# PSUM instead of SBUF for the gathered tokens' rows and sums and for the dense activations; three shared two-bank tiles for the sums over U and V

## The chip, the cores and the metric

One core of one Trainium2 chip runs the whole kernel. The metric is the device time of one execution in microseconds (us). Five engines work side by side, each with its own queue that it executes in order: TensorE (PE; its weight loads are listed as PEld), VectorE (DVE), ScalarE (ACT), GpSimd (POOL) and SyncE (SP), which only issues transfers. Sixteen DMA engines move data between HBM and SBUF. Matrix products are written to PSUM, which has eight banks of 128 partitions x 512 float32; DVE and ACT also read and write PSUM.

## What is computed

The reference is one decoder block over 1024 tokens of 1024 features: RWKV-7 time mixing and sparse attention side by side, merged through gates, a first LayerNorm, then a channel mixer (PEER) and a second LayerNorm. The change lies in PEER, which picks 128 of 16384 single-neuron experts for each token (8 heads x 16) and adds them up:

```
def chunk(args):                       # h2 rows, chosen experts, gates
    hc, ec, gc = args
    act = gelu(einsum('cd,chkd->chk', hc, u_tab[ec])) * gc
    return einsum('chk,chkd->cd', act, v_tab[ec])
x = layer_norm(ALPHA * x + gt2 * y2, ln2_g, ln2_b)
```

## The kernel before, in words

Instructions are written as Python generators over tiles; a planner then lays out the order of each engine's queue when the kernel is built, by its own costs of the instructions, and puts in the waits. A tile pool gives each name a fixed number of slots; an instruction that needs a slot waits until the last user of the slot's former tile is done.

Up to about 1650 us run the projections, RWKV, the attention and the first LayerNorm (twice, for 512 tokens each). Then come two stages in which PEER is computed in two ways at once:

- The 384 first tokens (NG = 3 tiles of 128) are **gathered** (`peer_gather`). For each of a token's 128 experts an indirect transfer, issued by POOL (L1366), brings one row of U per partition, 128 x 1024 float32, into a tile `g`, and DVE multiplies it with the tokens' rows `gh2` and sums (L1370) into one column of `dots`. After 128 such rows GELU and gates are applied, and 128 rows of V follow, which DVE adds up, each times its column of `dots`, into `gacc` (L1372 for the first, L1374 for the others). `g` has three slots, and one more (`g2`) in the last stage. `finish` multiplies `gacc` by gt2 (L1412), adds the residual (L1423), and normalizes. The U rows of tile 0 are taken before 1650 us, spread between RWKV's steps.
- The other 640 tokens (DN) are **dense**: they go through all 16384 experts, 128 at a time. `dots_u` multiplies a block of U with `h2T`; `dense_u` takes GELU (L1305, L1308), multiplies by the gates' table `gt` (L1309), and splits the result into a rounded part and the rest (a copy at L229, then L1312), `A`; `dense_v` multiplies eight of those by a block of V and adds to `yacc` (L1323). Each block of weights is loaded as `raw`, rounded by ACT (`whi`, L229), and POOL takes the rest (`wlo`, L1272). Products are made of three float32r matmuls per slice (`mm6`), for two halves of 320 tokens: 48 matmuls for each block.

The first of the two stages (about 1650 to 2395 us) is the retrieval of the tiles left and the tables of gates (`gate_table`, L1247, L1252), with V rows of the gathered tile 0, and with the products of 69 of the 128 blocks of U ("ahead"), which are stored in HBM (`dotD`). The second (about 2395 to 4007 us) is the dense part proper: groups of eight blocks of U, where the ahead ones come back from HBM into `al`, and the eight V products of the group before are emitted after the first four of a group. The gathered tiles 1 and 2 run beside it. After the last group `fin1` normalizes the dense tokens.

PSUM before is one pool for the whole kernel: `acc` two banks, `rw` four, `tp` two. A dense U block takes two `rw` banks until GELU has read them into `al` (SBUF); a V block takes one `acc` and one `tp` until L1323 has read them. So two U blocks and two V blocks have room at a time.

Of the kernel before, what the change touches and what calls it, by code (L numbers as in the profile page):

```python
# [8 lines left out]
F32 = mybir.dt.float32  # L9
F32R = mybir.dt.float32r  # L10
# [27 lines left out]
ONV = (2, 7)        # tiles whose scores are counted on VectorE  # L38
# [23 lines left out]
# candidate pairs (a, b) of ranks that can be among the 16 largest sums: (a+1)(b+1) <= 16  # L62
# [3 lines left out]
# ---------------------------------------------------------------- constants of the shapes alone  # L66
# [10 lines left out]
def _consts():  # L77
# [43 lines left out]
    # places where the ranks of the first key begin among the candidates, their differences, the ranks  # L121
# [26 lines left out]
def layout(i):  # L148
    """Data layout only: transposes, splits and joins of the inputs."""
# [55 lines left out]
def body(tc, a, out, dbg=None, ntiles=8, mark=lambda s: None):  # L205
# [25 lines left out]
    # ------------------------------------------------------------ modulation: first its part for h  # L231
# [10 lines left out]
    modc = base.tile([128, 48], F32, name="modc")     # sh1, 1 + sc1, gt1 / 2, shift and scale of h2, gt2  # L242
# [32 lines left out]
    def mod_rest(mp):  # L275
        """gt1 as columns; h2 = xn * scale + shift, as columns and as rows; gt2 as both."""
# [46 lines left out]
    def mod_row(dst, n):  # L323
        """The n-th row of shift and scale of h2, gt2, ALPHA times those of the first LayerNorm."""
# [3 lines left out]
    # ------------------------------------------------------------ constants, small parameters  # L328
# [40 lines left out]
        # rows of heads spread over their features, times the weights of the group norm  # L369
# [9 lines left out]
    # relative bias, negated and relative to the last bucket, as tiles over (query, key) of the last 256 keys  # L379
# [26 lines left out]
    def split_w(src, n):  # L406
        """A weight tile as the sums of pairs of float32r tiles, 512 columns each."""
# [11 lines left out]
    def proj(pt, w, act, nk):  # L419
        """pt[128 cols, n] = sum over k tiles, with weights and activations split in two."""  # L420
# [24 lines left out]
    xaD = [tc.dram_tile([128, 1024], F32, name=f"xaD{i}") for i in range(NGT)]  # L445
    h2D = [tc.dram_tile([128, 1024], F32, name=f"h2D{i}") for i in range(NGT)]
# [18 lines left out]
    def kv_index(H, act_of, zp, after=lambda: None):  # L465
        """c_kv, k_idx and w_idx (tokens on partitions) and q_idx; act_of(k) gives slice k of h, split in two."""
# [52 lines left out]
    def zphase1(H, hh, zp, side, pace):  # L519
        """Decay, gates and the rows of RWKV; pace steps of side are emitted after each column tile."""  # L520
# [5 lines left out]
        def shifted(j, dst):  # L526
            """Column tile j, mixed with the token before."""
# [10 lines left out]
        # decay (tokens on partitions), a, and what the output's gate is made of  # L538
# [13 lines left out]
        # k, r and v  # L552
# [35 lines left out]
        def norm():  # L588
            """kk over its norm, and what follows from it."""
# [14 lines left out]
    def spread():  # L604
        """What spreads rows of heads over their features."""
# [4 lines left out]
    def zphase2(H, act, js, side=iter(())):  # L610
        for j in js:
# [7 lines left out]
            else:  # L619
                # twice the sigmoid, less one  # L620
# [4 lines left out]
    anchors = [[], [], []]      # of RWKV for each half of the tokens and of the second merge: instructions of VectorE, in turn, that other work is queued behind  # L625
# [1067 lines left out]
```

## Time and profile before

| | |
|---|---|
| median of 3 runs | 4005.12 us (3998.66 to 4007.22) |
| span of the profiled execution | 4007.3 us |
| PE busy | 3605.5 us (90%), 24045 matmuls |
| DVE busy | 3036.1 us (76%) |
| POOL busy | 2236.6 us (56%) |
| ACT busy | 1618.8 us (40%) |
| moved by DMA | 924.65 MB, mean 231 GB/s |
| mean granted TensorE clock | 0.939 |

The span is that of one execution, from the first to the last instruction; no time of that execution besides its span was recorded. Busy time is the union of the engine's instructions; matmuls are pipelined, so a record of 310 ns can follow the one before after 147 ns. [...]

### The profile page before, as it was taken

Reading aid. Unit: us, or ns where it says so; the run is one execution under the profiler, and the core shown is the slowest. Engines: PE = TensorE matmul, PEld = TensorE weight load, DVE = VectorE, ACT = ScalarE, POOL = GpSimd, SP = SyncE. Lnnn points to the kernel's source line nnn. Section 1 sums busy time; section 2 is a strip of 40 time slices with the busy share of each in tenths; the row PEclk is TensorE's granted clock in tenths of the full one; section 3 lists DMA queues with packets and bytes.
Section 4 is the critical chain, followed back from the end, with each engine's and each line's share of the span. In section 5 each row is a group of like instructions: output and inputs, shape, how many; then the busy total and the mean of one; then the engine's idle time right before and its main releaser. Section 6 shows DMA issues by size and latency. Waiting matters only on the chain.

```text
span 4007.3 us, 65204 instructions
## 1 busy us (share of the span) xinstructions
PE 3605.5 (90%) x24045; PEld 3208.2 (80%) x24045; DVE 3036.1 (76%) x6103; ACT 1618.8 (40%) x3034; POOL 2236.6 (56%) x1566
## 2 busy tenths in 40 slices
PE   8698999888999998888988999999899999898997
PEld 6477776665777776678988889998899989898997
DVE  7556654857367758899999995887788877877874
ACT  3448942343444443564554654222222222222223
POOL 5342222345455543235455455777877777787775
PEclk9898998988999999889999999999999999999998
DMA  6463324855666665477777688888888888888873
GB/s 227 122 192 96 102 91 138 279 185 185 196 216 214 216 217 154 141 270 263 248 252 255 239 266 311 296 283 286 296 304 290 302 283 281 291 289 287 289 261 116
DMA packets 438172, 924.65 MB, mean 231 GB/s; under 512 B 36596, under 2 KB 198588, under 8 KB 434908
## 3 DMA queue, kind: packets, MB, share of 16 engines
q1 hardware_dynamic: 315132, 502.04, 38.1%
q0 software_dynamic: 122720, 418.43, 31.2%
q8 instruction: 190, 3.11, 0.3%
q14 instruction: 130, 1.06, 0.1%
HBM read 792.64 MB, written 127.68 MB: 230 GB/s over the span
## 4 chain that ended last, share of the span: by engine, by line
PE 39%; DVE 25%; DMA 14%; issue 10%; POOL 7%; ACT 3%; SPq 1%; POOLq 0%; DVEq 0%; ACTq 0%
DMA g<-in_u_dram,gidx 5%; PE acc L425 4%; PE acc L426 4%; PE acc L427 4%; DVE gacc L1374 4%; DVE g L1370 3%; POOL g L1366 3%; POOL wlo L1272 3%; DVE gt L1252 3%; DMA g<-in_v_dram,gidx 2%; DMA al<-dotD 2%; PE rw L1289 2%; PE rw L1287 2%; PE rw L1285 2%; PE acc L1287 2%
## 5 line engine op out<-in xcount | busy, mean ns | idle before, releaser
L1272 POOL TENSOR_TENSOR wlo<-raw,whi 128x1024 fp32r<-128x1024 f32 x264 | 662.2, 2509 | 162.2 <-ACT whi L229 156.0
L1366 POOL DMA_INDIRECT g<-in_v_dram,gidx x384 | 504.5, 1314 | 381.7 <-DVE gacc L1374 179.2
L415 POOL TENSOR_TENSOR wlo<-wraw,whi 128x512 fp32r<-128x512 f32 x280 | 374.3, 1340 | 606.2 <-ACT whi L229 537.2
L1370 DVE SCALAR_TENSOR_TENSOR g<-g,gh 128x1024 f32<-128x1024 f32 x384 | 570.5, 1505 | 173.6 <-DMA g<-in_u_dram,gidx 172.8
L1366 POOL DMA_INDIRECT g<-in_u_dram,gidx x384 | 509.4, 1326 | 343.6 <-DVE g L1370 210.0
L1374 DVE SCALAR_TENSOR_TENSOR gacc<-g,dots,gacc 128x1024 f32<-128x1024 f32 x381 | 602.5, 1581 | 113.9 <-DMA g<-in_v_dram,gidx 110.7
L229 ACT ACTIVATE whi<-raw 128x1024 fp32r<-128x1024 f32 x264 | 278.2, 1055 | 624.6 <-DMA raw<-in_ut_dram 192.9
L1289 PE MATMUL rw<-h2T,wlo 128*128 128x320 f32 x2048 | 479.8, 313 | 2.6 <-POOL wlo L1272 2.6
L1285 PE MATMUL rw<-h2T,whi 128*128 128x320 f32 x2048 | 478.5, 313 | 2.4 <-ACT ds L229 2.0
L1287 PE MATMUL rw<-h2T,whi 128*128 128x320 f32 x2048 | 479.3, 313 | 0.0
L1285 PE MATMUL acc<-A,whi 128*128 128x320 f32 (+2 forms) x1088 | 349.5, 321 | 65.0 <-ACT A L229 57.0
L425 PE MATMUL acc<-big,whi 128*128 128x512 f32 x864 | 359.9, 417 | 48.9 <-ACT whi L229 19.2
L1287 PE MATMUL acc<-A,whi 128*128 128x320 f32 (+2 forms) x1088 | 351.7, 323 | 52.4 <-DVE A L1312 52.4
L426 PE MATMUL acc<-big,whi 128*128 128x512 f32 x864 | 351.5, 407 | 4.4 <-DVE big L451 4.4
L427 PE MATMUL acc<-big,wlo 128*128 128x512 f32 x864 | 353.6, 410 | 1.4 <-POOL wlo L415 1.3
L1285 PEld LDWEIGHTS rw<-h2T,whi 128*128 128x128 f32 x2048 | 346.7, 190 | 5.4 <-ACT ds L229 2.5
L1289 PEld LDWEIGHTS rw<-h2T,wlo 128*128 128x128 f32 x2048 | 347.5, 190 | 4.3 <-POOL wlo L1272 3.1
L1289 PE MATMUL acc<-A,wlo 128*128 128x320 f32 (+2 forms) x1088 | 347.2, 319 | 1.9 <-POOL wlo L1272 1.9
L1287 PEld LDWEIGHTS rw<-h2T,whi 128*128 128x128 f32 x2048 | 347.1, 190 | 0.8
L229 ACT ACTIVATE whi<-wraw 128x512 fp32r<-128x512 f32 x280 | 175.3, 628 | 373.7 <-PE acc L426 141.2
L1287 PE MATMUL tp<-A,whi 128*128 128x320 f32 x960 | 306.8, 320 | 0.0
L1285 PE MATMUL tp<-A,whi 128*128 128x320 f32 x960 | 305.0, 320 | 2.0 <-DVE yacc L1323 2.0
(486 smaller groups left out, 7908.2 us busy)
## 6 DMA issues: line engine op xcount, KB each, us to landing
raw<-in_vt_dram SPq DMA_DIRECT2D x136, 512.0 KB
raw<-in_ut_dram SPq DMA_DIRECT2D x128, 512.0 KB
gtD<-st SPq DMA_DIRECT2D x20, 2048.0 KB
gt<-gtD SPq DMA_DIRECT2D x32, 1280.0 KB
wraw<-in_wz_dram SPq DMA_DIRECT2D x152, 256.0 KB
dotD<-ds SPq DMA_DIRECT2D x69, 320.0 KB
al<-dotD SPq DMA_DIRECT2D x69, 320.0 KB
mw<-in_wada_dram SPq DMA_DIRECT2D x32, 512.0 KB
```

What stands on the lines that cost most here:

```text
L229: copy = lambda o, i, **k: A.activation(o, i, AF.Copy, **k)
L415: G.tensor_tensor(lo, raw, hi.bitcast(F32), op=OP.subtract)
L425: mm(pt, lhsT=wh[:, ks], rhs=ah[:, k, :], start=k == 0, stop=False)
L426: mm(pt, lhsT=wh[:, ks], rhs=al[:, k, :], start=False, stop=False)
L427: ins = mm(pt, lhsT=wl[:, ks], rhs=ah[:, k, :], start=False, stop=k == nk - 1)
L1272: G.tensor_tensor(lo, raw, hi.bitcast(F32), op=OP.subtract)
L1285: mm(pts[n], lhsT=wh, rhs=ah[:, h], start=k == 0, stop=False)
L1287: mm(pts[n], lhsT=wh, rhs=al[:, h], start=False, stop=False)
L1289: mm(pts[n], lhsT=wl, rhs=ah[:, h], start=False, stop=last)
L1366: G.indirect_dma_start(out=u, out_offset=None, in_=a["u" if n < halves else "v"], in_offset=bass.IndirectOffsetOnAxis(ap=idx[:, k:k + 1], ...
L1370: V.scalar_tensor_tensor(u, u, 1.0, h2, op0=OP.mult, op1=OP.mult, accum_out=dots[:, k:k + 1])
L1374: V.scalar_tensor_tensor(acc, u, dots[:, k:k + 1], acc, op0=OP.mult, op1=OP.add)
```

## The change

The pool that held all of PSUM ends with the first part. From then on there are three others:

- `pg`, one two-bank tile, for the gathered tiles. It holds in turn the sum of the V rows (`acc`), from its first row until `finish` has multiplied it, and, for tiles 1 and 2, a copy (by ACT) of the tokens' rows, for their 128 U rows. Tile 0 reads its rows from SBUF as before.
- `ps2`, in the retrieval: `tp` two banks, and `pair` two tiles of two banks for the blocks that go to `dotD`, which one copy reads in place of two.
- `ps3`, in the dense part: `pair`, three tiles of two banks (PAIRS), shared by the U blocks, the V blocks, the ahead blocks and `fin1`. A U block stays in its pair through GELU (one instruction in place of two), gates, copy and subtraction; an ahead block takes a pair when GELU reads `al`. V's result is added to `yacc` by one instruction in place of two.

The case of a gathered part of a tile (GX, which was 0) and the comments are dropped.

```diff
-    ps = pool("ps", 2, space=PSUM)
     p1 = ExitStack()
+    banks = [p1.enter_context(tc.tile_pool(reuse_waits=REUSE, name="ps", bufs=2, space=PSUM))]
...
+    def ppair(bufs):
+        return banks[0].tile([128, 2, 512], F32, name="pair", bufs=bufs)
...
-    def dots_u(i1, du, h2T):
+    def dots_u(i1, du, h2T, bufs):
         uh, ul = split2(du, a["ut"][i1])
-        pts = [prw()[:, 0:DN // 2] for _ in HALVES]
+        pt = ppair(bufs)[:, :, 0:DN // 2]
+        pts = [pt[:, n, :] for n in range(2)]
...
     def dense_u(i1, du, dv, h2T, act, gt):
...
-        al = dv.tile([128, DN], F32, name="al", bufs=ALB)
         if i1 in ahead:
+            al = dv.tile([128, DN], F32, name="al", bufs=ALB)
             nc.sync.dma_start(al, dotD[ahead[i1]])
-            A.activation(al, al, AF.Gelu)
+            pt = ppair(PAIRS)[:, :, 0:DN // 2]
+            A.activation(pt, by_half(al), AF.Gelu)
         else:
-            for pt, h in zip(dots_u(i1, du, h2T), HALVES):
-                A.activation(al[:, h], pt, AF.Gelu)
-        V.tensor_tensor(al.rearrange(...), al.rearrange(...), gt[:, :, i1 % 4, :], op=OP.mult)
-        copy(hi, al)
-        V.tensor_tensor(lo, al, hi.bitcast(F32), op=OP.subtract)
+            pt = dots_u(i1, du, h2T, PAIRS)
+            A.activation(pt, pt, AF.Gelu)
+        pt4 = pt.rearrange("p h (a b) -> p h a b", b=32)
+        V.tensor_tensor(pt4, pt4, gt[:, :, i1 % 4, :].rearrange(...), op=OP.mult)
+        copy(by_half(hi), pt)
+        V.tensor_tensor(by_half(lo), pt, by_half(hi.bitcast(F32)), op=OP.subtract)
...
     def dense_v(g, d, du, act, yacc, halves=HALVES):
-        pts = [p()[:, 0:h.stop - h.start] for p, h in zip((pacc, ptp), halves)]
+        pt = ppair(PAIRS)
+        pts = [pt[:, n, 0:h.stop - h.start] for n, h in enumerate(halves)]
...
-        for pt, h in zip(pts, halves):
-            V.scalar_tensor_tensor(yacc[:, d, h], pt, modc[:, 40 + d:41 + d], yacc[:, d, h], ...)
+        src, dst = pts[0], yacc[:, d, halves[0]]
+        if len(halves) == 2:
+            src, dst = pt[:, :, 0:DN // 2], by_half(yacc[:, d, :])
+        V.scalar_tensor_tensor(dst, src, modc[:, 40 + d:41 + d], dst, ...)
...
-    def peer_gather(i, du, dv):
+    def peer_gather(i, du, dv, pg):
...
+        if i > 0:
+            hp = pg.tile([128, 1024], F32, name="pg")
+            copy(hp, h2)
+            h2 = hp
-        acc = gp.tile([128, 1024], F32, name="gacc")
...
+            if n == 2:
+                acc = pg.tile([128, 1024], F32, name="pg")
...
-    def finish(i, y2, dv, rows):
+    def finish(i, acc, dv, rows):
...
-            V.tensor_tensor(y2, y2, row, op=OP.mult)
+        y2 = gp.tile([128, 1024], F32, name="gacc")
+        V.tensor_tensor(y2, acc, row, op=OP.mult)
...
     with tc.tile_pool(reuse_waits=REUSE, name="du", bufs=1) as du, \
+            tc.tile_pool(reuse_waits=REUSE, name="pg", bufs=1, space=PSUM) as pg:
...
-                for pt, h in zip(dots_u(i1, du, h2T), HALVES):
-                    copy(ds[:, h], pt)
+                copy(by_half(ds), dots_u(i1, du, h2T, 2))
```

## Rows read from the trace of the kernel before

**Rows 1.** Busy time by stage; columns: stretch, us, engines, clock, DMA share, GB/s

```profile
0.00:1650.00 1650.00, 1476.78 (x10090) 1133.63 (x10091) 1063.93 (x2823) 789.64 (x1708) 673.47 (x633) 0.93 0.56 174
1650.00:2395.00 745.00, 664.67 (x4407) 633.76 (x4406) 730.92 (x1917) 392.32 (x716) 365.05 (x229) 0.95 0.74 253
2395.00:3950.00 1555.00, 1431.40 (x9313) 1409.51 (x9312) 1214.37 (x1322) 421.81 (x592) 1166.05 (x687) 0.95 0.84 285
```

**Rows 2.** Groups by line and shape, 2395 to 3950; busy, mean ns | idle

```profile
L1374 DVE SCALAR_TENSOR_TENSOR gacc<-g,dots,gacc 128x1024 f32<-128x1024 f32 x254 | 422.8, 1665 | 113.5 <-DMA g<-in_v_dram,gidx 110.5
L1370 DVE SCALAR_TENSOR_TENSOR g<-g,gh 128x1024 f32<-128x1024 f32 x238 | 383.2, 1632 | 123.2 <-DMA g<-in_u_dram,gidx 123.0
L1366 POOL DMA_INDIRECT g<-in_v_dram,gidx x256 | 352.4, 1377 | 130.4 <-DVE gacc L1374 79.8 <-issue 35.1 <-DVE yacc L1323 6.7
L1366 POOL DMA_INDIRECT g<-in_u_dram,gidx x235 | 329.9, 1404 | 159.3 <-DVE g L1370 91.3 <-issue 27.5 <-DVE al L1309 9.1
...
L1312 DVE TENSOR_TENSOR A<-al,A 128x640 fp32r<-128x640 f32 x128 | 144.2, 1127 | 12.3 <-ACT A L229 11.9 <-issue 0.3
L1309 DVE TENSOR_TENSOR al<-al,gt 128x640 f32<-128x640 f32 x128 | 128.5, 1004 | 52.3 <-ACT al L1305 39.3 <-ACT al L1308 13.0
L229 ACT ACTIVATE A<-al 128x640 fp32r<-128x640 f32 x128 | 94.6, 739 | 493.8 <-DVE al L1309 486.1 <-DVE g L1370 4.4 <-issue 3.0
```

**Rows 3.** Timeline, 2998 to 3006: start, us, engine, line, operation; PE left out

```profile
2998.07 3.94 DVE L1374 SCALAR_TENSOR_TENSOR gacc<-g,dots,gacc 128x1024 f32<-128x1024 f32 x1
2998.53 2.39 POOL L1272 TENSOR_TENSOR wlo<-raw,whi 128x1024 fp32r<-128x1024 f32 x1
...
3002.28 0.95 POOL L1366 DMA_INDIRECT g<-in_v_dram,gidx  x1 [1.36 <-DVE gacc L1374]
...
3004.10 2.42 POOL L1272 TENSOR_TENSOR wlo<-raw,whi 128x1024 fp32r<-128x1024 f32 x1 [0.86 <-ACT whi L229]
...
3005.54 1.65 DVE L1309 TENSOR_TENSOR al<-al,gt 128x640 f32<-128x640 f32 x1 [1.48 <-ACT al L1305]
```

**Rows 4.** Single lines, 2395 to 3950: duration ns min/median/max, first and last start

```profile
L1374 DVE SCALAR_TENSOR_TENSOR gacc<-g,dots,gacc x254: 1268/1285/4018, 2770.5 to 3892.4; 128x1024 f32<-128x1024 f32 x127
...
L1323 DVE SCALAR_TENSOR_TENSOR yacc<-acc,modc,yacc x127: 533/543/619, 2554.1 to 3948.0; 128x320 f32<-128x320 f32 x120, 128x384 f32<-128x384 f32 x7
...
L1366 POOL DMA_INDIRECT g<-in_v_dram,gidx x256: 932/1291/2013, 2758.6 to 3886.7; - x128
...
L1272 POOL TENSOR_TENSOR wlo<-raw,whi x194: 2349/2421/3426, 2400.1 to 3946.2; 128x1024 fp32r<-128x1024 f32 x194
```

**Rows 5.** Who waited for whom, 2395 to 3950: total us, times, longest

```profile
ACT A L229 <- DVE al L1309: 486.1, 115, 10.8
...
DVE g L1370 <- DMA g<-in_u_dram,gidx: 123.0, 60, 10.6
...
DVE gacc L1374 <- DMA g<-in_v_dram,gidx: 110.5, 67, 5.1
...
PE acc L1285 <- ACT A L229: 57.0, 18, 6.3
PE acc L1287 <- DVE A L1312: 52.4, 26, 4.2
```

**Rows 6.** Timeline of PE: the first and last of eight successive matmuls

```profile
2999.48 0.31 PE L1285 MATMUL acc<-A,whi 128*128 128x320 f32 x1
...
3000.51 0.31 PE L1285 MATMUL tp<-A,whi 128*128 128x320 f32 x1
```

**Rows 7.** Groups by line and shape, 1650 to 2395

```profile
L1374 DVE SCALAR_TENSOR_TENSOR gacc<-g,dots,gacc 128x1024 f32<-128x1024 f32 x127 | 179.7, 1415 | 0.4 <-DMA g<-in_v_dram,gidx 0.2
```

**Rows 8.** Timeline of DVE where the gather goes from tile 1 to 2

```profile
3142.10 1.23 DVE L1412 TENSOR_TENSOR gacc<-gacc,g 128x1024 f32<-128x1024 f32 x1
...
3152.80 1.22 DVE L1370 SCALAR_TENSOR_TENSOR g<-g,gh 128x1024 f32<-128x1024 f32 x1
```

**Rows 9.** Busy time of a stretch of 200 us, columns as in rows 1

```profile
2400.00:2600.00 200.00, 187.65 (x1273) 184.45 (x1272) 143.91 (x204) 75.65 (x122) 131.39 (x79) 0.98 0.86 302
```

More of the change, by code (lines that the diff above doesn't have):

```diff
@@ L51 @@
 NG = 3
-GX = 0
-TD = NG * 128 + GX
+TD = NG * 128
 DN = 1024 - TD
 CUT = 384
-NGT = NG + (GX > 0)
+PAIRS = 3
 BIG = 1.0e30
@@ L218, in pacc @@
     def pacc():
-        return ps.tile([128, 512], F32, name="acc", bufs=2)
+        return banks[0].tile([128, 512], F32, name="acc", bufs=2)
     def prw():
-        return ps.tile([128, 512], F32, name="rw", bufs=4)
+        return banks[0].tile([128, 512], F32, name="rw", bufs=4)
     def ptp(dt=F32):
-        return ps.tile([128, 512], dt, name="tp", bufs=2)
+        return banks[0].tile([128, 512], dt, name="tp", bufs=2)
+    def ppair(bufs):
+        return banks[0].tile([128, 2, 512], F32, name="pair", bufs=bufs)
     mm = nc.tensor.matmul
@@ L444, in body @@
         ybD[H] = tc.dram_tile([8, 128, 512], F32, name=f"ybD{H}")
-    xaD = [tc.dram_tile([128, 1024], F32, name=f"xaD{i}") for i in range(NGT)]
-    h2D = [tc.dram_tile([128, 1024], F32, name=f"h2D{i}") for i in range(NGT)]
+    xaD = [tc.dram_tile([128, 1024], F32, name=f"xaD{i}") for i in range(NG)]
+    h2D = [tc.dram_tile([128, 1024], F32, name=f"h2D{i}") for i in range(NG)]
     xaT = tc.dram_tile([128, 8, DN], F32, name="xaT")
@@ L1083, in merge @@
                 G.dma_start(h2TD[:, n, :, dst], h2T[:, n, :, c0:])
-        for tt, xn in enumerate(xns[:max(0, NGT - 4 * H)]):
+        for tt, xn in enumerate(xns[:max(0, NG - 4 * H)]):
             i = H * 4 + tt
@@ L1321, in dense_v @@
             mm6(pts, vh[:, ks], vl[:, ks], ah, al, k, k == 7, halves)
-        for pt, h in zip(pts, halves):
-            V.scalar_tensor_tensor(yacc[:, d, h], pt, modc[:, 40 + d:41 + d], yacc[:, d, h], op0=OP.mult, op1=OP.add)
+        src, dst = pts[0], yacc[:, d, halves[0]]
+        if len(halves) == 2:
+            src, dst = pt[:, :, 0:DN // 2], by_half(yacc[:, d, :])
+        V.scalar_tensor_tensor(dst, src, modc[:, 40 + d:41 + d], dst, op0=OP.mult, op1=OP.add)
     def grow(bufs=GB):
         return gp.tile([128, 1024], F32, name="g", bufs=bufs)
-    def rows_in(dst, src, n, c):
-        for r in range(128 // n):
-            at = 0 if src.shape[1] == c else r * c
-            nc.sync.dma_start(dst[r * n:r * n + n, 0:c], src[0:n, at:at + c])
     def behind(row):
@@ L1402, in out_rows @@
         nc.sync.dma_start(out[r0:r0 + n, :], dst[p])
-    def finish(i, y2, dv, rows):
-        n = 128 if i < NG else GX
-        p = slice(0, n)
-        last = i == NGT - 1
+    def finish(i, acc, dv, rows):
+        last = i == NG - 1
         row, xa = ((dv.tile([128, 2 * DN], F32, name="A", bufs=AB)[:, 0:1024] if last else grow()) for _ in range(2))
         mod_row(row, 2)
-        if n == 128:
-            V.tensor_tensor(y2, y2, row, op=OP.mult)
-        else:
-            sel = gp.tile([128, 1024], F32, name="gh2")[:, 0:n]
-            V.tensor_reduce(sel, ident.rearrange("p (s t) -> p t s", t=n), axis=AX.X, op=OP.add)
-            for h, pt in enumerate((ptp(), prw())):
-                hs = slice(512 * h, 512 * h + 512)
-                mm(pt[p], lhsT=sel, rhs=y2[:, hs], start=True, stop=True)
-                V.tensor_tensor(row[p, hs], row[p, hs], pt[p], op=OP.mult)
-            y2 = row
-        nc.sync.dma_start(xa[p], xaD[i][p])
-        V.tensor_tensor(y2[p], y2[p], xa[p], op=OP.add)
+        y2 = gp.tile([128, 1024], F32, name="gacc")
+        V.tensor_tensor(y2, acc, row, op=OP.mult)
+        nc.sync.dma_start(xa, xaD[i])
+        V.tensor_tensor(y2, y2, xa, op=OP.add)
         g, b = rows[0:2] if last else (grow(), grow())
@@ L1439, in fin1 @@
             n = min(128, c1 - c)
-            v = [prw(), prw()]
+            pt = ppair(PAIRS)
+            v = [pt[:, h, :] for h in range(2)]
             for d in range(8):
@@ L1609, in body @@
         mark("retr1")
-        with tc.tile_pool(reuse_waits=REUSE, name="slots", bufs=1) as sl:
+        with tc.tile_pool(reuse_waits=REUSE, name="slots", bufs=1) as sl, \
+                tc.tile_pool(reuse_waits=REUSE, name="ps2", bufs=2, space=PSUM) as banks[0]:
             st = sl.tile([128, 2, 128, 32], F32, name="st")
@@ L1639, in body @@
         mark("dense")
-        with tc.tile_pool(reuse_waits=REUSE, name="dv", bufs=1) as dv:
+        with tc.tile_pool(reuse_waits=REUSE, name="dv", bufs=1) as dv, \
+                tc.tile_pool(reuse_waits=REUSE, name="ps3", bufs=PAIRS, space=PSUM) as banks[0]:
             yacc = dv.tile([128, 8, DN], F32, name="yacc")
@@ L1669, in body @@
             mark("gather")
-            for i in range(NGT):
-                finish(i, peer_gather(i, du, dv), dv, ln)
+            for i in range(NG):
+                finish(i, peer_gather(i, du, dv, pg), dv, ln)
     mark("end")
```

31 lines of the change are left out of this document (14 added, 17 removed).

## The prediction

> **What bounds the kernel now.** I read the busy times by stage first [rows 1]. Up to 1650 us nothing that the change touches is at work except one pool's opening, so I take that part as unchanged. In the retrieval, DVE is busy 731 of 745 us: it sets that stage. In the dense stage nobody is full: PE 1431 of 1555, DVE 1214, POOL 1166, DMA 0.84 of its share at 285 GB/s. PE comes nearest, so the next question is what PE lacks there.
>
> How much there is to win: eight successive matmuls start from 2999.48 to 3000.51, 147 ns apart [rows 6], so a block of 48 takes 7.06 us. The stage holds 59 U blocks (128 less the 69 ahead) and 128 V blocks: 187 x 7.06 = 1320 us of 1555. [...]
>
> The waits say who ends the idle time [rows 5]: PE waited 57.0 us for the rounded half of `A` (ACT) and 52.4 us for the rest of it (DVE), together 109 of the 124. ACT in turn waited 486.1 us, in 115 waits, for L1309: 4.2 us each, up to 10.8. So the path that sets the stage runs GELU, L1309 on DVE, copy on ACT, L1312 on DVE, first matmuls of a V product, and it is DVE's queue that is late.
>
> Why it is late is in the groups [rows 2] and in one stretch of the timeline [rows 3]. L1374 takes 1665 ns in the mean and 1285 in the median, up to 4018 [rows 4]. The long ones lie on POOL's subtraction: the L1374 that starts at 2998.07 ends at 3002.01, 1.09 us after the `wlo` of 2998.53 has ended (3000.92), as if its work stood still meanwhile; the L1309 of 3005.54 takes 1.65 us, and ends 0.67 us after the `wlo` that ran from 3004.10 to 3006.52. Both have two inputs in SBUF. L1323, which reads one input from PSUM and one from SBUF, lies beside the same `wlo`s and never takes more than 619 ns, its longest form included [rows 4]. The reverse holds too: POOL's issue of an indirect transfer takes 932 ns at the least, 1291 in the median and 2013 at the most [rows 4]; the one of 3002.28, with no such DVE instruction beside it, took 0.95 [rows 3]. So DVE with two SBUF inputs and POOL stop each other, and the change takes the second SBUF input from nearly every DVE instruction of the dense stage.
>
> **Part by part, dense stage.** The trace shows no DVE instruction that writes PSUM, and no ACT one. Reading PSUM is shown by L1323: 543 ns for 320 columns, at most 619 for 384, hence 1.2 ns for each further column at most; 1024 would be 543 + 704 x 1.2 = 1390 at the dear end, and L1374's minimum, 1268, is the cheap end [rows 4]. I take 1300, nearer to the cheap end: from L1323 to L1374's median the step is (1285 - 543) / 704 = 1.05 ns a column, and the 619 is the largest of seven of another shape. For 640 columns I take 1.1 ns: 543 + 320 x 1.1 = 895.
> - V rows: 254 x (1665 - 1300) = 93 us off DVE. U rows of tiles 1 and 2: 238 x (1632 - 1300) = 79 us [rows 2].
> - Gates and subtraction: 128 x (1004 - 895) + 128 x (1127 - 895) = 14 + 30 us [rows 2].
> - `yacc`: two instructions of 543 become one of 895, 120 times: 23 us [rows 4].
> - DVE together 239 us, 1214 to 975.
> - POOL: 256 x (1377 - 950) + 235 x (1404 - 950) = 109 + 107 = 216 us, 1166 to 950 [rows 2, 3]. If these did not shorten, POOL would still have a quarter of the stage free.
> - ACT: one GELU in place of two, and two copies of 128 x 1024 for tiles 1 and 2. I cost both at nothing: ACT is busy 422 of 1555 us [rows 1]. Without that cover the copies are about 1.2 us each (739 ns for 640 columns [rows 2]). The first V row of a tile (L1372) is one instruction a tile, and left out.
>
> [...]
>
> What is DVE's relief worth to PE? DVE's queue is in order, and it also stands still while a gathered row lands: 123.0 + 110.5 = 233 us [rows 5]. Busy and standing together it is taken 1447 of 1555 us, 93%; after, 975 + 233 = 1208, 78%. What a newcomer such as L1309 waits in a queue goes roughly with taken / free: 13 before, 3.5 after, a quarter. I count two thirds of the 109 us, not three quarters, because the gathered rows' landings stay in the queue: 73 us. Of the 71 us of low clock, which follow on PE's idling, I count a quarter: 18. Dense stage: -91 us. The bounds: nothing, if the landings alone make `A` late; and all of 109 + 71 = 180.
>
> A check from the side of the transfers: 1555 us at 285 GB/s are 443 MB; in 1464 us they need 303 GB/s, and one stretch of 200 us had 302 [rows 9]. So the sum asks for no rate that is not there, but hardly for less than the best.
>
> **Retrieval.** L1374 here: 127 x (1415 - 1300) = 15 us [rows 7], passed on in full since DVE is busy 98%. Bounds: -3 (1390 ns) to -19 (1268). The blocks for `dotD` keep room for two, the tables keep `tp`; `acc`, which goes, is unused there.
>
> **New waits.** The one `pg` tile is passed from the sum of tile 1 to the rows of tile 2: the copy on ACT can start when L1412 has ended, and the first U row waits for it, with all that stands behind it in DVE's queue. Before, L1412 starts at 3142.10 and the first U row comes at 3152.80 [rows 8], because the slots of `g` that `finish` takes hold up the gather; 10.7 us cover a multiplication of 1.3 us, a copy of 1.2 us, and their waits. So nothing; about 3 us at each of two places if the cover is gone. `finish` issues the same transfers from SP as before, so SP's queue gains none.
>
> The three pairs cost nothing in the mean: a U block holds one for 7.06 us of matmuls, then GELU (taken as the copy's 0.74), 4.2 for L1309, 0.74 for the copy and about 1.1 for L1312 [rows 2, 5], 14 us; an ahead block 7, a V block 8. A group (8 V, 3.7 U, 4.3 ahead) asks for 64 + 52 + 30 = 146 us of pairs, 49 for each of three, and takes 1555 / 16 = 97 us.
>
> **Sum.** -91 - 15 = -106 us. The profiled span, 4007.3 us, is 2.2 above the median (and is all that is recorded of that execution), so I set 4005 - 106 = 3899 us.
>
> **Rivals.**
> 1. *The landings set the pace.* DVE's 233 us of waiting for gathered rows grow as DVE gets faster, and L1309 stands behind the same landings. For it: DMA share 0.84, and rows still arrive one 512 KB transfer at a time through the same slots. Against it: POOL's issue and DVE's release, both shortened, are two parts of each slot's round. Only the retrieval's 15 us remain, and some 5 of the shorter DVE instructions in `A`'s path: 3985.
> 2. *PE reaches its floor.* All the waits for `A` and the low clock go: 4005 - 180 - 15 = 3810. For it, DVE and POOL both get over 200 us of room; against it, 443 MB in 1375 us want 322 GB/s.
> 3. *The pairs run out* (the other side). Before, two U and two V blocks had room, and a U block's banks were free after GELU. Now three pairs stand for four, and are held through three more instructions, and a GELU that waits for a pair stands in ACT's queue before the next `whi`. It decides when a U block holds its pair beyond three blocks of PE, 21 us, which needs DVE 10 us late: the longest wait for L1309 was 10.8 [rows 5], the mean 4.2. Each block that then waits 1 us costs 187 us over the stage; from 0.57 us a block (106 / 187) on it eats the gain, and at 1 us the time is 4005 - 106 + 187 = 4086. A new order of the queues by the planner, with GELUs early, would do the same.
> 4. *Gain and pair waits cancel:* 4005.
>
> **How the numbers follow.** Forecast 0.50 (by itself 3840 to 3960), rival 1 0.15, rival 2 0.12, rival 3 0.15, rival 4 0.08. About 0.2%, 8 us, is what a measurement of this kernel tells from no change. So faster 0.77, same 0.08, slower 0.15. The range, 3790 to 4020, takes in rivals 1, 2 and 4 and leaves out most of 3 and the tails.
>
> **What would show it.** Right: in the dense stage L1374's and L1370's successors have means near their medians, 1.25 to 1.4 us, with no tail to 4 us; the indirect issues fall to about 0.95; DVE falls below 1050 us; PE's waits for `A` fall to some 40 us; DMA passes 300 GB/s. Wrong: L1374 well over 1.4 us with nothing beside it (writing PSUM is dear), PE or ACT waiting for the release of `pair` for tens of us, or the same dense stage with longer waits of DVE for `g`.

## The result and the profile after

The changed kernel takes 3897.81 us in the median of four executions, against 4006.17 for the kernel before in the same set: -108 us where -106 was forecast, and a ratio of 0.9713 with a 95% interval of [0.9688, 0.9739]. One of the four, 4036.69 us at a granted clock of 0.814, counts in that median but not in the ratio; the median of the other three is 3895.00. The profiled execution spans 3893.1 us (before 4007.3), -114.2.

The busy times by stage, kernel after (columns as in [rows 1]; its dense stage ends some 110 us earlier, so the last stretch is shorter):

```profile
0.00:1650.00 1650.00, 1470.31 (x10078) 1129.95 (x10079) 1065.59 (x2822) 790.69 (x1707) 676.54 (x633) 0.93 0.55 174
1650.00:2395.00 745.00, 664.40 (x4412) 636.77 (x4411) 687.72 (x1787) 367.56 (x610) 357.63 (x240) 0.95 0.75 257
2395.00:3840.00 1445.00, 1389.13 (x9351) 1379.80 (x9349) 989.78 (x1344) 440.59 (x577) 928.43 (x679) 0.99 0.85 305
```

The first stage is as it was. In the dense stage DVE is busy 225 us less, POOL 238 less; PE idles 1445 - 1389 = 56 us (124 before) at a clock of 0.99 (0.95). In the retrieval DVE is busy only 688 us up to 2395, where it was 731. It did not have less to do: it got through 1787 instructions in place of 1917, and stood idle longer.

Where the stages meet can be read from the first multiplication by the gates, 128 of which make up the dense stage. In single lines of the kernel before and of the one after (duration in ns, minimum/median/maximum, then the first and last start):

```profile
L1309 DVE TENSOR_TENSOR al<-al,gt x128: 805/817/2514, 2493.4 to 3919.3; 128x640 f32<-128x640 f32 x128
```

```profile
L1319 DVE TENSOR_TENSOR pair<-pair,gt x128: 817/826/833, 2517.5 to 3801.6; 128x640 f32<-128x640 f32 x128
```

It comes at 2517.5 instead of 2493.4: 24.1 us *later*. From there to the end of the span it is 1375.6 us instead of 1513.9 ("the dense part" below): -138.3. So the total of -114 is a larger gain than forecast, less a loss that was not forecast. The dense part of the kernel before and of the one after, columns as in [rows 1]:

```profile
2493.40:4007.30 1513.90, 1371.76 (x8909) 1350.80 (x8907) 1180.29 (x1260) 388.92 (x530) 1146.15 (x673) 0.94 0.82 278
```

```profile
2517.50:3893.10 1375.60, 1323.16 (x8926) 1317.22 (x8924) 909.81 (x1130) 383.85 (x473) 919.16 (x671) 0.98 0.85 305
```

For about as many matmuls (8926 and 8909) PE is busy 49 us less, at a clock of 0.98 for 0.94, and it idles 52 us for 142, which is 90 less. The granted clock is 1.0 or 0.5 at any one time in these traces: 0.5 for 178.6 us of the dense part before and 42.2 us of the one after. In the kernel before, successive matmuls of 320 columns start 267 ns apart at 0.5 (2548.74, 2549.01, 2549.27) and 147 ns apart at 1.0 (2559.80, 2559.95, 2560.10). In the lines of L1309 and L1319, the tail up to 2514 ns is gone: 833 at most.

The groups of the dense stage after, which answer to [rows 2]:

```profile
L1383 DVE SCALAR_TENSOR_TENSOR pg<-g,dots,pg 128x1024 f32<-128x1024 f32 x254 | 326.4, 1285 | 145.4 <-DMA g<-in_v_dram,gidx 131.9 <-issue 9.6 <-DVE pg L1383 1.6
L1379 DVE SCALAR_TENSOR_TENSOR g<-g,pg 128x1024 f32<-128x1024 f32 x229 | 276.8, 1216 | 117.9 <-DMA g<-in_u_dram,gidx 115.7 <-issue 0.2
L1375 POOL DMA_INDIRECT g<-in_v_dram,gidx x256 | 241.0, 941 | 126.5 <-DVE pg L1383 66.7 <-issue 35.5 <-DMA g<-in_v_dram,gidx 14.7
L1375 POOL DMA_INDIRECT g<-in_u_dram,gidx x227 | 216.5, 954 | 138.4 <-DVE g L1379 70.8 <-issue 29.2 <-DMA gidx<-idxD 13.4
...
L1335 DVE SCALAR_TENSOR_TENSOR yacc<-pair,modc,yacc 128x640 f32<-128x640 f32 x120 | 105.6, 880 | 47.2 <-PE pair L1293 43.7 <-issue 1.6 <-PE pair L1291 1.5
L1321 DVE TENSOR_TENSOR A<-pair,A 128x640 fp32r<-128x640 f32 x128 | 104.1, 819 | 44.2 <-ACT A L233 44.2
```

The means of the long lines now lie on the former medians: 1285 for 1665, 1216 for 1632, 819 for 1127. Single lines show how flat they are now (the largest values in [rows 4] were 4018 and 2013):

```profile
L1383 DVE SCALAR_TENSOR_TENSOR pg<-g,dots,pg x254: 1276/1287/1292, 2766.2 to 3770.1; 128x1024 f32<-128x1024 f32 x127
L1375 POOL DMA_INDIRECT g<-in_v_dram,gidx x256: 932/938/955, 2755.0 to 3759.1; - x128
```

The waits of the dense stage after (who waited for whom: total us, times, longest), against [rows 5]:

```profile
ACT A L233 <- DVE pair L1319: 172.4, 82, 6.9
DVE pg L1383 <- DMA g<-in_v_dram,gidx: 131.9, 94, 5.6
DVE g L1379 <- DMA g<-in_u_dram,gidx: 115.7, 84, 6.9
ACT pair L1314 <- DVE A L1321: 69.3, 26, 5.5
ACT pair L1314 <- DVE yacc L1335: 43.2, 16, 4.9
PE pair L1289 <- DVE A L1321: 20.3, 11, 4.2
```

ACT's wait for the gates fell from 486.1 to 172.4 us. ACT's waits for a free pair (L1314, 112 us) are new. The last line is new too, and it is not a wait for `A`: L1289 reads only the rounded half of `A`, which ACT makes (L233), while L1321 is the last reader of a pair. So PE waits there for a pair, at the start of a block; the longest of these waits stands between a U block and a V block:

```profile
3363.97 0.46 PE L1293 MATMUL pair<-h2T,wlo 128*128 128x320 f32 x2
3368.66 0.53 PE L1289 MATMUL pair<-A,whi 128*128 128x320 f32 x2 [4.24 <-DVE A L1321]
```

Of PE's waits for `A`, 109 us before, 1.6 are left, on the matmuls with the rest of `A` (L1291):

```profile
L1291 PE MATMUL pair<-A,whi 128*128 128x320 f32 x1920 | 440.9, 311 | 2.2 <-DVE A L1321 1.6 <-issue 0.6
```

The loss ahead of the dense part stands in the timeline of DVE after: two successive instructions at the start of the retrieval (start, us, ..., idle time before and who ended it):

```profile
1660.22 0.23 DVE L1225 CAST idx<-i 128x128 uint32<-128x128 f32 x1
1699.18 0.87 DVE L1140 MAX8 v<-sc 128x8 f32<-128x128 f32 x4 [38.73 <-ACT sc L233]
```

DVE, which sets this stage, has nothing to do for 38.7 us: ACT's copy of the scores comes late, since the score matmuls (L1131) start on PE only at 1698.0, behind the projections of the queries, the last of which starts at 1697.7. Those scores are in `tp`, in the pool that is opened new for this stage.

### The profile page after: what moved, and what is told of

The parts are those of the page before. It is cut to its first block, busy times and chain, and to the rows that moved or that the text cites. A ratio compares the mean times of both kernels' runs of the same rounds, so it can differ in the third digit from the quotient of the medians.

```text
span 3893.1 us, 65065 instructions
## 1 busy us (share of the span) xinstructions
PE 3552.1 (91%) x24045; PEld 3174.2 (82%) x24045; DVE 2761.7 (71%) x5983; ACT 1611.3 (41%) x2909; POOL 1989.5 (51%) x1566
## 3 DMA queue, kind: packets, MB, share of 16 engines
q14 instruction: 128, 1.05, 0.1%
## 4 chain that ended last, share of the span: by engine, by line
PE 41%; DVE 20%; DMA 16%; POOL 9%; issue 8%; ACT 4%; SPq 1%; POOLq 0%; ACTq 0%; DVEq 0%
PE pair L1289 5%; PE pair L1291 5%; PE pair L1293 5%; PE acc L429 4%; PE acc L430 4%; PE acc L431 4%; POOL g L1375 4%; POOL wlo L1276 4%; DMA g<-in_v_dram,gidx 3%; DMA raw<-in_ut_dram 3%; DVE pg L1383 3%; DVE gt L1256 3%; DMA g<-in_u_dram,gidx 3%; DMA raw<-in_vt_dram 2%; DVE g L1379 2%
## 5 line engine op out<-in xcount | busy, mean ns | idle before, releaser
L1383 DVE SCALAR_TENSOR_TENSOR pg<-g,dots,pg 128x1024 f32<-128x1024 f32 x381 | 488.5, 1282 | 154.1 <-DMA g<-in_v_dram,gidx 140.4
L233 ACT ACTIVATE whi<-raw 128x1024 fp32r<-128x1024 f32 x264 | 278.6, 1056 | 710.0 <-PE pair L1291 366.4
L1289 PE MATMUL pair<-A,whi 128*128 128x320 f32 (+2 forms) x2048 | 482.4, 312 | 25.8 <-DVE A L1321 20.3
L1289 PE MATMUL pair<-h2T,whi 128*128 128x320 f32 x2048 | 478.8, 314 | 14.0 <-DMA h2T<-h2TD 11.1
L1291 PE MATMUL pair<-h2T,whi 128*128 128x320 f32 x2048 | 481.6, 314 | 3.6 <-DMA h2T<-h2TD 3.6
L1291 PE MATMUL pair<-A,whi 128*128 128x320 f32 (+2 forms) x2048 | 481.5, 311 | 2.2 <-DVE A L1321 1.6
L1293 PE MATMUL pair<-A,wlo 128*128 128x320 f32 (+2 forms) x2048 | 480.2, 311 | 2.5 <-POOL wlo L1276 2.5
L1293 PE MATMUL pair<-h2T,wlo 128*128 128x320 f32 x2048 | 480.2, 314 | 0.3 <-POOL wlo L1276 0.3
L1379 DVE SCALAR_TENSOR_TENSOR g<-g,pg 128x1024 f32<-128x1024 f32 x256 | 308.8, 1215 | 118.8 <-DMA g<-in_u_dram,gidx 116.4
L1289 PEld LDWEIGHTS pair<-A,whi 128*128 128x128 f32 x2048 | 348.8, 190 | 28.9 <-issue 20.1
L1289 PEld LDWEIGHTS pair<-h2T,whi 128*128 128x128 f32 x2048 | 348.7, 191 | 15.4 <-issue 11.3
L1291 PEld LDWEIGHTS pair<-h2T,whi 128*128 128x128 f32 x2048 | 349.2, 191 | 5.4 <-DMA h2T<-h2TD 3.9
L1291 PEld LDWEIGHTS pair<-A,whi 128*128 128x128 f32 x2048 | 349.2, 190 | 3.8 <-DVE A L1321 2.8
L1293 PEld LDWEIGHTS pair<-A,wlo 128*128 128x128 f32 x2048 | 348.7, 190 | 3.0 <-POOL wlo L1276 3.0
L1293 PEld LDWEIGHTS pair<-h2T,wlo 128*128 128x128 f32 x2048 | 348.2, 191 | 2.0 <-POOL wlo L1276 0.5
```

The lines of the kernel that those rows point to most:

```text
L233: copy = lambda o, i, **k: A.activation(o, i, AF.Copy, **k)
L1289: mm(pts[n], lhsT=wh, rhs=ah[:, h], start=k == 0, stop=False)
L1291: mm(pts[n], lhsT=wh, rhs=al[:, h], start=False, stop=False)
L1293: mm(pts[n], lhsT=wl, rhs=ah[:, h], start=False, stop=last)
L1379: V.scalar_tensor_tensor(u, u, 1.0, h2, op0=OP.mult, op1=OP.mult, accum_out=dots[:, k:k + 1])
L1383: V.scalar_tensor_tensor(acc, u, dots[:, k:k + 1], acc, op0=OP.mult, op1=OP.add)
```

## Experiments

Two theories at the start. *Lock* (a name for what [rows 3] shows, a DVE instruction of 1285 ns that takes 3.94 us beside POOL's subtraction; by what means the engines do it, no run shows): DVE instructions with two inputs in SBUF and POOL's instructions stop each other, and the change takes the second SBUF input away. *Rivals:* fewer and longer instructions in the dense chain, or another order of the queues, bring the time, whatever lies in PSUM. The planner lays out every run's queues anew, so the readings below rest on the lengths of instructions and on named waits more than on totals. For each run there is the ratio to the kernel before, from runs on the same chip, with a 95% interval in brackets.

### e1: the gathered rows and their sum back in SBUF

```
-        if i > 0:
-            hp = pg.tile([128, 1024], F32, name="pg")
-            copy(hp, h2)
-            h2 = hp
...
-                acc = pg.tile([128, 1024], F32, name="pg")
+                acc = gp.tile([128, 1024], F32, name="gacc")
```

> The changed kernel with the gathered rows and the running sum back in SBUF (no pg tile); the dense activations and the three pairs stay. If the gain comes from DVE and POOL no longer stopping each other at the gather (492 long DVE instructions, as many indirect issues), L1374's and L1370's successors go back to about 1.6 us in the dense stage, the indirect issues to about 1.35, and most of the gain goes: 3960 to 3990 us. If it comes from the dense side (fewer instructions, activations in PSUM) or from a luckier order of the queues, the time stays at 3895 to 3920.

Measured 4006.54 us, 0.9992 [0.9977, 1.0006]: nothing is left of the gain, and the time is 17 us above the range that was expected. Groups of e1, 2500 to 3700:

```profile
L1375 DVE SCALAR_TENSOR_TENSOR g<-g,gh 128x1024 f32<-128x1024 f32 x212 | 378.4, 1802 | 90.2 <-DMA g<-in_u_dram,gidx 90.0
L1379 DVE SCALAR_TENSOR_TENSOR gacc<-g,dots,gacc 128x1024 f32<-128x1024 f32 x188 | 350.6, 1865 | 77.0 <-DMA g<-in_v_dram,gidx 75.0
...
L1289 PE MATMUL pair<-A,whi 128*128 128x320 f32 x1664 | 391.4, 317 | 77.3 <-DVE A L1321 75.2 <-ACT A L233 2.1
```

The rows do not go back to the 1632 (U) and 1665 (V) of [rows 2], but to 1802 and 1865. The lines of the gates and of the subtraction, left in PSUM, stay flat in this run (means of 822 and 814). So what these two paid before, the rows now pay as well. And PE waits 75 us at L1289 for a pair: with DVE's queue late, the activations hold their pairs longer. The loss at the start of the retrieval is in this kernel too (first gates at 2520.6); the dense part is 1477.8, 36 us shorter than before. The fewer, longer instructions of the dense chain and the new pools are all in e1, and while the rows lie in SBUF they bring no more than that. What they are worth without the lock, e4 and e8 show.

### e2: the dense activations back in SBUF

```
+        al = dv.tile([128, DN], F32, name="al", bufs=ALB)
...
-            pt = dots_u(i1, du, h2T, PAIRS)
-            A.activation(pt, pt, AF.Gelu)
+            A.activation(by_half(al), dots_u(i1, du, h2T, PAIRS), AF.Gelu)
+        pt = by_half(al)
```

> The changed kernel with GELU's result, its multiplication by the gates and the split back in SBUF (al), so that a U block leaves its pair after GELU; the gather stays in PSUM, V and U still share three pairs. If the lock matters on the path of A itself, gates and subtraction lie behind wlo again in some 100 of 256 cases, up to 2.4 us each, and the time rises by 20 to 50 us: 3915 to 3945. If the pairs, held longer, are what costs now, it falls or stays: 3870 to 3900.

Measured 3975.10 us, 0.9917 [0.9894, 0.9941]: slower than expected, 77 us above the changed kernel. Groups of e2, 2500 to 3700:

```profile
L1382 DVE SCALAR_TENSOR_TENSOR pg<-g,dots,pg 128x1024 f32<-128x1024 f32 x199 | 255.4, 1284 | 67.1 <-DMA g<-in_v_dram,gidx 64.8
...
L1318 DVE TENSOR_TENSOR al<-al,gt 128x640 f32<-128x640 f32 x111 | 206.4, 1860 | 81.8 <-ACT al L1313 51.5 <-DMA gt<-gtD 17.7 <-ACT al L1315 12.6
L1320 DVE TENSOR_TENSOR A<-al,A 128x640 fp32r<-128x640 f32 x111 | 143.5, 1293 | 11.6 <-ACT A L233 11.6
...
L1289 PE MATMUL pair<-A,whi 128*128 128x320 f32 x1676 | 394.4, 317 | 59.1 <-ACT A L233 59.1
```

The gates, 1004 ns in [rows 2], now take 1860: each pays 1034 over its undisturbed 826, where it paid 187 over 817. A U block frees its pair after GELU here, and PE waits for `A` itself again (59 us), for a pair no more. So the lock is not a fixed price for each DVE instruction. It goes with POOL's subtractions, and whichever two-input instruction meets one pays. The timeline of the kernel before shows it one by one, 2843 to 2849, DVE and POOL:

```profile
2843.59 1.28 DVE L1374 SCALAR_TENSOR_TENSOR gacc<-g,dots,gacc 128x1024 f32<-128x1024 f32 x1
2844.50 3.37 POOL L1272 TENSOR_TENSOR wlo<-raw,whi 128x1024 fp32r<-128x1024 f32 x1
2844.78 0.82 DVE L1312 TENSOR_TENSOR A<-al,A 128x640 fp32r<-128x640 f32 x1
2845.52 3.44 DVE L1374 SCALAR_TENSOR_TENSOR gacc<-g,dots,gacc 128x1024 f32<-128x1024 f32 x1
```

The first L1374 and L1312 take their usual time, and the subtraction that came upon them takes 3.37 us in place of 2.42. The second L1374 begins while it runs, and ends 1.09 us after it. Of the 702 instructions of the four two-input lines that start between 2520 and 3900, the 514 that overlap no subtraction are at most 0.08 us above their medians; the 147 lengthened by more than 0.3 us end 0.68 to 1.10 us after a subtraction. Worked out for POOL's subtractions: in [rows 2] the four two-input lines lie 254 x (1665 - 1285) + 238 x (1632 - 1216) + 128 x (1004 - 817) + 128 x (1127 - 819) = 259 us over their undisturbed durations (those of the changed kernel, and 817), 1.3 us for each of 194 subtractions; in e1 212 x (1802 - 1216) + 188 x (1865 - 1285) = 233 us, 1.5 for each of 151; in e2 111 x (1860 - 826) + 111 x (1293 - 819) = 167, 1.1 for each of 154.

### e6: only the sum of the V rows back in SBUF

The second half of e1's edit.

> The changed kernel with only the running sum of the V rows back in SBUF; the tokens' rows for the U rows of tiles 1 and 2 stay in PSUM. If POOL's subtraction stops whatever DVE instruction with two SBUF inputs is left, the sum's instructions take 1.8 to 1.9 us in the mean in the stretches of V rows, more than the 1.67 of the kernel before, and those of the U rows 1.22; about half of the gain goes: 3940 to 3965 us. If prices add up by instruction, the sum's are at 1.67 and the time is 3925 to 3945.

Measured 3966.35 us, 0.9892 [0.9864, 0.992]. Groups of e6, 2500 to 3700:

```profile
L1383 DVE SCALAR_TENSOR_TENSOR gacc<-g,dots,gacc 128x1024 f32<-128x1024 f32 x200 | 378.5, 1893 | 80.8 <-DMA g<-in_v_dram,gidx 78.8
L1379 DVE SCALAR_TENSOR_TENSOR g<-g,pg 128x1024 f32<-128x1024 f32 x212 | 256.0, 1216 | 111.5 <-DMA g<-in_u_dram,gidx 106.4 <-issue 3.7 <-DVE yacc L1335 0.5
```

One line left in SBUF, of four, takes 1893 ns, longer than when there were four (1665), and costs 69 us of the 108: 200 x (1893 - 1285) = 122 us of lengthening, 0.8 for each of POOL's subtractions (about as many as in e2). So it is less with one line to pay, but more than what that line paid when there were four: 254 x (1665 - 1285) = 97 us, 0.5 for each of 194. PE's waits at L1289 for a pair are back as well (60 us of the same stretch). The time is 1 us above what was expected, the duration as expected.

### e4: the kernel before, POOL's subtraction taken away

The kernel leaves out the subtraction: `wlo` is a plain copy by ACT.

```
-        G.tensor_tensor(lo, raw, hi.bitcast(F32), op=OP.subtract)
+        copy(lo, raw)
```

> The kernel before, with wlo made by ACT as a plain copy of raw in place of POOL's subtraction (that part of the computation is left out); POOL is left with the indirect issues alone, everything else is in SBUF as before. If POOL's subtraction is what lengthens DVE's instructions with two SBUF inputs, L1374's mean in the dense stage falls from 1665 to about 1290 ns with no tail to 4 us, the indirect issues still take 1.3 us and more beside DVE, and the time falls by 40 to 100 us: 3905 to 3965. If the length has another cause (the rows' landing in SBUF, PE's reads), the mean stays above 1500 and the time near 4000.

Measured 3752.9 us, 0.9368 [0.9345, 0.939], far below the range. Groups of e4, 2500 to 3700, nothing of it in PSUM that was not before:

```profile
L1374 DVE SCALAR_TENSOR_TENSOR gacc<-g,dots,gacc 128x1024 f32<-128x1024 f32 x254 | 325.4, 1281 | 100.6 <-DMA g<-in_v_dram,gidx 98.3
L1366 POOL DMA_INDIRECT g<-in_v_dram,gidx x256 | 312.7, 1221 | 345.6 <-DVE gacc L1374 285.0 <-DMA g<-in_v_dram,gidx 32.0 <-issue 16.8
```

The same instruction in the same place falls from 1665 to 1281 ns as soon as POOL no longer subtracts. That is the lock, without the change. The four lines shown under e2 agree with it. POOL's indirect issues still lengthen (1221 for 941 after), but do not lengthen DVE's instructions in turn (L1374's 1281 beside them). The dense part is 1332.2 us (first gates at 2410.0), about the 1320 that the prediction worked out from 187 blocks of 7.06 us, and it starts 83 us earlier. So the subtraction also stops the retrieval's DVE instructions, most of which the change left as they were: between 1650 and 2395 DVE is busy 652 us with 2028 instructions, where it was 731 with 1917, and the tables' L1252 takes 347 ns in the mean for 464, L1247 1213 for 1284. The time of e4 is not the lock's alone, though: without the subtraction POOL's queue is free for the issues too.

### e8: the changed kernel with `tp` kept (e3's edit) and no subtraction (e4's)

> The kernel with tp kept, and wlo made by ACT as a plain copy of raw (the subtraction is left out), so that POOL only issues. With the activations and the gather in PSUM the dense part has hardly any instruction that POOL could stop, so there this should change little: PE was busy 98% of it. What it gains it gains in the retrieval, whose tables still have two SBUF inputs: 40 to 70 us, 3775 to 3805. If the dense part was still held by POOL in another way (the subtraction's own 2.4 us before the issue of a row, say), it goes to the 3750 of the kernel before with the same substitution, or below.

Measured 3738.49 us, 0.9332 [0.9309, 0.9354]: below 3775 to 3805, at the level that was given for a dense part still held by POOL in another way. Busy times of e8, 2600 to 3600, and of the changed kernel in the same stretch:

```profile
2600.00:3600.00 1000.00, 1000.00 (x6821) 1000.00 (x6820) 721.00 (x846) 415.80 (x490) 368.99 (x393) 1.00 0.94 336
```

```profile
2600.00:3600.00 1000.00, 980.86 (x6629) 977.41 (x6628) 695.48 (x871) 275.68 (x337) 686.00 (x514) 0.99 0.90 324
```

PE has no gap at full clock: the dense part, 1332.9 us, is that of e4. So with the lock gone neither PSUM nor the fewer, longer instructions add anything to the dense part, and PE is its floor; the changed kernel is some 43 us above it. Against e3, which differs by the subtraction alone, the first gates come 70 us earlier and the dense part is 35 us shorter (1368.0 in e3). There DVE's instructions were flat already, but its waits for gathered rows (2500 to 3700) fall from 246 us to 63. That POOL's subtractions stand before the issues of these rows is a likely cause of the 35 us, not a shown one.

### e3: `tp` in a pool of its own, kept to the end of the retrieval

```
+    tps = ExitStack()
+    tpp = tps.enter_context(tc.tile_pool(reuse_waits=REUSE, name="tpp", bufs=2, space=PSUM, side="right"))
...
-        return banks[0].tile([128, 512], dt, name="tp", bufs=2)
+        return tpp.tile([128, 512], dt, name="tp", bufs=2)
...
+        tps.close()
```

> The changed kernel with the two tp banks in a pool of their own from the start to the end of the retrieval, so that only acc and rw are given up at the end of the first part. The trace of the changed kernel has DVE idle for 38.7 us from 1660 on, in front of the first scores of the retrieval. If these scores wait for banks of the pool that ends, that idle time goes, the gate tables no longer outlast the blocks that go to HBM, and the time falls by 20 to 40 us: 3860 to 3880. If PE's projections simply come first in PE's queue by the planner's order, nothing changes: 3890 to 3905.

Measured 3844.45 us, 0.9596 [0.9574, 0.9619]: 53 us less than the change, more than expected. Busy times of 1650 to 1750, of the changed kernel and of e3:

```profile
1650.00:1750.00 100.00, 81.57 (x414) 70.60 (x413) 53.92 (x245) 29.19 (x46) 44.91 (x34) 0.87 0.74 256
```

```profile
1650.00:1750.00 100.00, 80.95 (x458) 68.41 (x458) 92.96 (x322) 56.19 (x103) 36.40 (x25) 0.91 0.66 234
```

DVE gets its 39 us back there, and the first gates come at 2465.9 instead of 2517.5, 51.6 us earlier: that is the gain. The retrieval's late start came from the change of pools between the stages. PE did not stand and wait for the banks meanwhile: from 1660 to 1698 it is busy 36.3 of 38 us in the changed kernel, with the projections, while e3 has score matmuls among them (at 1652.72). So what is late is the scores' place in PE's queue. Why the planner gave them that place when the pool changes, no run shows.

### e7: two pairs instead of three

`PAIRS = 2`, nothing else.

> The changed kernel with two shared pairs in place of three in the dense part. By the working of the prediction a group of the dense part asks for 146 us of pairs; of three it needs 49 us, of two 73, of a group's 85 us in the changed kernel. If the third pair is only slack, the time rises by 0 to 30 us: 3900 to 3930. If the pairs are near their limit, PE waits for pairs at every change between U and V, some 3 to 6 us at 187 blocks' ends taken together with GELU: 200 us and more, 4100 to 4500.

Measured 3990.95 us, 0.9958 [0.9941, 0.9974], between the two. Waits of e7, 2500 to 3700 ("issue" is time in which the engine waited for nothing that the profile shows):

```profile
ACT whi L233 <- issue: 263.1, 59, 11.9
...
PEld pair L1289 <- issue: 89.0, 21, 9.7
PE pair L1289 <- DVE A L1321: 87.6, 25, 9.5
```

L1383 is flat here too (1285), and yet 93 us are lost: with two pairs a U block that holds its pair through GELU, gates, copy and subtraction leaves PE without a pair for 87.6 us (20.3 with three, over 2395 to 3840). That it is the pair is plainest where the next block is a U block, which reads no `A`: 6.3 of the 87.6 us. The lock's removal is worth something here only while there is a pair for the next block.

### e5, e9, e10: the blocks ahead

e5 is e3 with the subtraction of the 69 blocks ahead on DVE, although DVE sets the stage in which they are made:

```
-        G.tensor_tensor(lo, raw, hi.bitcast(F32), op=OP.subtract)
+        (eng or G).tensor_tensor(lo, raw, hi.bitcast(F32), op=OP.subtract)
...
-                copy(by_half(ds), dots_u(i1, du, h2T, 2))
+                copy(by_half(ds), dots_u(i1, du, h2T, 2, V))
```

> The kernel with tp kept, and the subtraction that makes wlo done by DVE instead of POOL for the 69 blocks of U that are multiplied in the retrieval. Each costs DVE about 1.2 us, 83 us in all, in a stage that DVE fills. If each of POOL's subtractions stops DVE for as long as it runs, or nearly, as soon as one DVE instruction with two SBUF inputs or in the fast one-input form stands at the head of the queue, 63 subtractions of 2.6 us in that stage cost DVE more than that: the retrieval gets shorter by 20 to 60 us and the time is 3790 to 3830. If DVE loses only the 0.15 us a piece that the means of the tables' instructions show over their best, some 60 to 90 us in all, it is a draw or worse: 3840 to 3870.

Measured 3814.86 us, 0.9515 [0.9487, 0.9542], 30 us below e3. Groups of DVE in the retrieval, 1650 to 2395, of e3 and of e5:

```profile
L1258 DVE TENSOR_SCALAR gt<-iotan,slots 128x128 f32<-128x128 f32 x453 | 189.0, 482 | 0.0
```

```profile
L1258 DVE TENSOR_SCALAR gt<-iotan,slots 128x128 f32<-128x128 f32 x426 | 118.8, 344 | 0.0
...
L1278 DVE TENSOR_TENSOR wlo<-raw,whi 128x1024 fp32r<-128x1024 f32 x69 | 84.0, 1217 | 9.6 <-ACT whi L235 7.4 <-issue 1.2 <-ACT st L235 1.0
```

DVE takes on 84 us of subtractions, and L1258, an instruction with *one* SBUF input, falls from 482 to 344 ns, 426 x 138 = 59 us back on that line alone; L1253, with two inputs, falls from 1308 to 1215. So POOL's subtraction holds up this form with one input too. Of what the expectation calls the fast one-input form the kernel before has an instruction of 1024 columns: L1372 takes 743 ns in the median, where L1374 takes 1285.

e9 (`EXTRA = 16`, 75 blocks ahead) and e10 (`J0 = 5`, `EXTRA = 7`, 81 ahead) use DVE's room in the retrieval for more of them.

> The kernel with tp kept and DVE's wlo for the ahead blocks, with 75 blocks ahead in place of 69. In that kernel the ahead blocks end at 2354 us and the tables at 2424, and PE is busy 98.5% of the dense part: six blocks of 7.06 us moved from the dense part into room that PE has in the retrieval give 42 us at the best, less 1.2 us of DVE each there: 3775 to 3800. If the retrieval is as long as DVE makes it, and the dense part by now waits for rows and weights rather than for PE, nothing: 3805 to 3825.

> As the run with 75 blocks, with 81: twelve blocks, 85 us at the best, of which some 15 go to DVE in the retrieval. If PE still has room there, 3745 to 3780; if the ahead blocks now outlast the tables, it is like the one with 75 or worse: 3785 to 3820.

Measured 3788.98 us, 0.9453 [0.9423, 0.9484], within what was expected, and 3788.23, 0.9447 [0.9425, 0.9468]. Six blocks more shorten e5's dense part by 39 us (6 x 7.06 = 42), and it starts 6 us later; the next six take 31 us off it and delay its start by 28. Here it levels off. These two are the fastest kernels that leave nothing out: 109 us below the changed kernel.

## Why the prediction was right, and where it was not

- **The bound and the lock.** Right, and now shown from both sides: e4 takes POOL's part away, and e1, e2 and e6 put DVE's back.
- **The price of one instruction.** Predicted 1300 for 1024 columns and 895 for 640; measured 1285 and 1216, 819 to 880. DVE's relief was 225 us for 239, in a stretch 110 us shorter, POOL's 238 for 216. The prediction's ground for 1300, the 1.05 ns a column from L1323's 543 to L1374's 1285, was weak, since two points always lie on one line; the runs decide it. No added time for reading PSUM shows where one of two inputs moved there: medians of 1287 after and 1285 before in the V rows, 826 and 817 in the gates.
- **How it was split among the parts: the step that failed in form.** The prediction gave each line a price of its own, 172 us for the rows and 44 for gates and subtraction, and added them. In the dense part e1, with the gates' half of the change alone, gains 1513.9 - 1477.8 = 36 us; e2, with the rows' half alone, 1513.9 - 1460.6 = 53; both together gain 138, not 89. The lines that are left pay for POOL's subtractions, and in e1 PE waits 75 us for pairs that are held longer. The sum came out because the change takes all four lines away.
- **What relief is worth to PE.** Mis-sized: -138 for -91. In the dense part PE idles 90 us less (-73 predicted) and is busy 49 us less for as many matmuls (-18 predicted). The waits for `A` went almost wholly, 109 us to 1.6, not by two thirds, and 20 us of waits for a pair are new. With the idle time down from 142 to 52 us the granted clock rose from 0.94 to 0.98; that is more than the quarter of the low clock that was counted. No run shows the 71 us of low clock of which that quarter is taken; they were the author's estimate. What the trace before shows for the dense part is 19 stretches at 0.5, 178.6 us in all, and PE busy for 4 to 42% of the 3.4 us ahead of each.
- **Retrieval.** Wrong in sign: instead of -15 the dense part starts 24 us later. L1374's successor did fall, from 1415 to 1276 ns, which is 18 us, but that was not passed on. From 1650 to the first gates DVE is busy 786 us in place of 792, as other lines lengthened (one `TENSOR_TENSOR`, L1194, now L1198, from 732 to 964 ns, another, L1207, now L1211, from 190 to 980), and it idles 81 us in place of 52. In e3, without the late scores, the first gates come 27.5 us earlier than in the kernel before.
- **New waits.** The three pairs were counted at nothing in the mean; PE waits 20 us for them. The hand-over of `pg` shows among no wait of PE. The pools' hand-over at the start of the retrieval was not looked at beyond "one pool's opening". It costs 38.7 us of DVE, on the stage that DVE sets, and 53 us in all (e3).
- **Rival 1 (landings)** fell: DVE's waits for rows, 233 us, became 248, and DMA moved 305 GB/s over the whole stage, where the stretch of [rows 9] had 302. **Rival 2 (PE's floor)** is where e4 and e8 end, and the changed kernel comes within 43 us of it in the dense part. **Rival 3 (pairs)** is at work with 20 us of PE's waits; with two pairs (e7) it takes most of the gain, so the margin is one pair. The two errors, -47 and +39 us, nearly cancel. That the total lands on the forecast is luck: e3, the change without the late scores, is at 3844.45, 55 us below the forecast.

Left open: an exact split of all blocks without POOL was not tried, so how much of e4's 3752.9 us such a kernel could reach is not known; nor why the planner puts the first scores behind the projections when the pool changes; nor how much of e4's and e8's gain is the lock's, and how much that of a POOL queue without subtractions.

## What to carry over

Where two engines hold each other up, as POOL and DVE do here (L1374 takes 1665 ns beside POOL's subtractions and 1281 without them), count the price by the instructions of the one that holds the other up (0.8 to 1.5 us for each subtraction in the kernel before, e1, e2 and e6), and ask which lines are left to pay: the two halves of this change gained 36 and 53 us of 138 in the dense part. A tile that was moved to PSUM for its lines' sake also held its banks longer here, with 112 us of ACT's waits and 20 of PE's: look at who waits for the banks, and read a wait by what the waiting instruction can need. When tiles move to other pools, follow the first user of the new pool in each stage, above all in a stage whose bound is another engine. And a step that moves work onto the busier engine can still gain, if it ends a lock that lengthens other instructions there: in e5 DVE took on 84 us of subtractions, and L1258 fell from 482 to 344 ns.

## What had not been expected of the hardware

- The lengthening does not stay with a line: the gates' 1004 ns became 1860 when the rows' lines left SBUF, and the V rows' 1665 became 1893.
- POOL's issue of an indirect transfer took 1221 ns in e4, where VectorE's instructions have two SBUF inputs, and 941 after, where they have one; VectorE's V rows did not lengthen with it: they took 1281 in e4 and 1285 after.
- With two inputs, VectorE writes PSUM at the pace of SBUF here: medians of 1287 (L1383) and 1285 ns (L1374) for 1024 columns. With one input it does not: L1372 took 743 ns into SBUF, and its successor L1381 takes 1277 into PSUM. ScalarE's GELU of 640 columns from SBUF took 705 ns into two banks of PSUM (L1314), and 731 within SBUF in the kernel before (L1305).
